# Reciprocal root on Pool: one power instruction and one Newton step in place of the bit trick and three steps

## The chip, the cores and the metric

The kernel runs on one core of a Trainium2 chip. The metric is the device time of one execution in microseconds (us). A trace covers a little less than that: the span of the profiled execution of the kernel before is 319.7 us, its time 321.52. A ratio is the mean time of one kernel's fast runs over that of the other's of the same rounds, so it is not quite the ratio of the medians that stand beside it.

## The reference

```python
x: [8, 1024, 2048] float32; gamma, beta: [2048]; eps = 1e-5
mean = np.mean(x, axis=-1, keepdims=True)
var = np.var(x, axis=-1, keepdims=True)
out = gamma * (x - mean) / np.sqrt(var + eps) + beta
return 0.5 * out * (1 + np.tanh(np.sqrt(2 / np.pi) * (out + 0.044715 * out ** 3)))
```

There are 8192 rows, so 64 tiles of 128 rows. x is 67.1 MB and the output is as large.

## The kernel before

The tiles go through in 22 groups, the first of one tile and the others of three. One load brings a group (3 MiB), one store takes it away. Seven group buffers are loaded ahead. A later load goes out on the SyncE queue right after a store, when the store before that one has landed in memory, because it reuses that buffer (in the trace of before SyncE waits for such a landing 14 times, 125.0 us in all).

```python
def scalar_var(i):                   # first tile of a group: statistics on ScalarE
    sq = gsmall.tile([P, 1], F32, name="sq")
    nc.scalar.activation(out=junk, in_=xts[i], func=ACTF.Square, bias=slot(i)[:, 0:1], accum_out=sq, ...)
    nc.gpsimd.tensor_scalar(out=slot(i)[:, 1:2], in0=sq, scalar1=1.0 / d, scalar2=None, op0=MUL)   # L136

def group_chain(g):                  # 1/sqrt(var + eps) and sqrt(var + eps) of three tiles, on Pool
    po = nc.gpsimd
    po.tensor_scalar(out=ve, in0=mvs[g][:, :, 1], scalar1=float(eps), scalar2=None, op0=ADD)
    po.tensor_scalar(out=y[:].bitcast(I32), in0=ve[:].bitcast(I32), scalar1=-0.5,
                     scalar2=float(0x5F3759DF), op0=MUL, op1=ADD)
    for _ in range(3):               # Newton: y = y * (1.5 - 0.5 * ve * y * y)
        po.tensor_tensor(out=t, in0=y, in1=y, op=MUL)
        po.tensor_tensor(out=t, in0=t, in1=ve, op=MUL)
        po.tensor_scalar(out=t, in0=t, scalar1=-0.5, scalar2=1.5, op0=MUL, op1=ADD)
        po.tensor_tensor(out=y, in0=y, in1=t, op=MUL)
    po.tensor_tensor(out=std, in0=ve, in1=y, op=MUL)

def diagonal(j): ...                 # ScalarE: w = identity * std, waits for the chain (L160)
def affine(j): ...                   # VectorE: ps = (x - mean) * gamma (L166); TensorE: ps += w @ beta (L169)
def gelu(j): ...                     # ScalarE: x = gelu(y * ps) (L178), then the store (L186; last group L184, L181)
```

The other two tiles of a group get their statistics on VectorE (`bn_stats`, L123). VectorE's statistics of later groups stand in program order between the affine instructions of earlier ones.

Of the kernel before, what the change touches and what calls it, by code (L numbers as in the profile page):

```python
# [7 lines left out]
F32 = mybir.dt.float32  # L8
BF16 = mybir.dt.bfloat16
I32 = mybir.dt.int32  # L10
ACTF = mybir.ActivationFunctionType
MUL = mybir.AluOpType.mult
ADD = mybir.AluOpType.add
SUB = mybir.AluOpType.subtract
P = 128
# [4 lines left out]
def kernel(  # L20
# [10 lines left out]
    nc = tc.nc  # L31
# [8 lines left out]
    singles = ctx.enter_context(tc.tile_pool(name="singles", bufs=1))  # L40
# [12 lines left out]
    for b, i in enumerate(starts):  # L53
        m = R if i else 1
# [25 lines left out]
    for b in range(NB):  # L80
# [6 lines left out]
    ident = singles.tile([P, P], F32)  # L87
    nc.gpsimd.affine_select(out=ident, in_=ones, pattern=[[-1, P]], base=0, channel_multiplier=1,
                            compare_op=mybir.AluOpType.is_equal, fill=0.0)
    H = d // 2  # L90
    halves = [slice(h * H, (h + 1) * H) for h in range(2)]
    ps = [[psum.tile([P, H], F32, name=f"ps{k}{h}") for h in range(2)] for k in range(2)]
    for pts, row in zip(ps, (g_t, b_t)):
        for pt, s in zip(pts, halves):
            for c in range(0, H, BANK):
                nc.tensor.matmul(pt[:, c:c + BANK], lhsT=ones[0:1, :],  # L96
# [41 lines left out]
    def group_chain(g):  # L138

        m = groups[g]  # L140
        ve = gsmall.tile([P, m], F32, name="ve")
        y = gsmall.tile([P, m], F32, name="y")
        t = gsmall.tile([P, m], F32, name="t")
        std = gsmall.tile([P, m], F32, name="std")
        po = nc.gpsimd
        po.tensor_scalar(out=ve, in0=mvs[g][:, :, 1], scalar1=float(eps), scalar2=None, op0=ADD)  # L146
        po.tensor_scalar(out=y[:].bitcast(I32), in0=ve[:].bitcast(I32), scalar1=-0.5,  # L147
                         scalar2=float(0x5F3759DF), op0=MUL, op1=ADD)
        for _ in range(3):
            po.tensor_tensor(out=t, in0=y, in1=y, op=MUL)  # L150
            po.tensor_tensor(out=t, in0=t, in1=ve, op=MUL)  # L151
            po.tensor_scalar(out=t, in0=t, scalar1=-0.5, scalar2=1.5, op0=MUL, op1=ADD)  # L152
            po.tensor_tensor(out=y, in0=y, in1=t, op=MUL)  # L153
        po.tensor_tensor(out=std, in0=ve, in1=y, op=MUL)  # L154
        rstds[g] = (y, std)

# [6 lines left out]
    def affine(j):  # L163
        g, k = of_tile[j]
        for pt, s in zip(ps[j % 2], halves):
            nc.vector.scalar_tensor_tensor(out=pt, in0=xts[j][:, s], scalar=mvs[g][:, k, 0:1],  # L166
                                           in1=g_t[:, s], op0=ADD if j in on_scalar else SUB, op1=MUL)
            for c in range(0, H, BANK):
                nc.tensor.matmul(pt[:, c:c + BANK], lhsT=wts[j], rhs=b_t[:, s.start + c:s.start + c + BANK],  # L169
# [28 lines left out]
    for j in range(ntiles):  # L198
        g, k = of_tile[j]
        target = min(len(chunks), max(pos, done_at[g] + AFTER[k]))  # L200
        while pos < target:
            i, c = chunks[pos]
            chunk(i, c)
            pos += 1
            h = of_tile[i][0]
            if done_at[h] == pos:
                while passes and of_tile[passes[0][1]][0] <= h:
                    f, q = passes.pop(0)
                    f(q)
                group_chain(h)  # L210
        if k == 0:
            for q in range(groups[g]):
                diagonal(j + q)
        affine(j)
        if j > 0:
            gelu(j - 1)
        now = of_tile[chunks[min(pos, len(chunks) - 1)][0]][0]
        if passes and of_tile[passes[0][1]][0] <= now and k != 1:
            f, q = passes.pop(0)
            f(q)  # L220
# [36 lines left out]
```

## Time and profile before

| | before |
|---|---|
| median of the first runs | 321.75 us (321.65 to 321.97, 4 runs) |
| bytes moved | 134.38 MB, 420 GB/s over the span |
| chain of fifteen Pool instructions | 7.95 us |
| pace of compute, one group of three tiles | 13.33 us |
| last load landed | 274.5 us |
| last gelu ends | 311.1 us |
| last store landed | 318.2 us |

One column of a view of windows needs care. The DMA share is a mean over the core's sixteen DMA engines, so a share below 1 doesn't say whether all of them had a pause or a few of them a long one.

### The profile page before, as it was taken

To read this page: it belongs to the slowest core of one execution; us is meant where nothing else is said; L and a number is where in the kernel's file an instruction comes from. 1 tells how busy PE (TensorE), PEld (TensorE's weight loads), DVE (VectorE), ACT (ScalarE), POOL (GpSimd) and SP (SyncE) were. 2 spreads that over 40 slices of the span, in tenths; PEclk is the share of its full clock that TensorE was granted. 3 is DMA by queue.
4 is the path that set the end of the run, shared out by engine and by line. 5 is a ranking of instruction groups with operands and counts; after the bars stand their busy time and mean duration, and the time that the engine had idled before them with its cause. 6 is when DMAs were issued, how large, how long until landed. Compare 5 with 4: busy or idle time off the path is not lost.

```text
span 319.7 us, 2374 instructions
## 1 busy us (share of the span) xinstructions
PE 253.1 (79%) x528; PEld 104.0 (33%) x528; DVE 269.1 (84%) x344; ACT 238.6 (75%) x282; POOL 149.6 (47%) x356
## 2 busy tenths in 40 slices
PE   5982979869896696968969869896696966869670
PEld 2421424324333242333424324333242322324230
DVE  2677799999999999999999999999999989798420
ACT  2363978869797696977968869797696976968560
POOL 0305346373463734637346383563835638365300
PEclk9998789997999999979989997999999999999995
DMA  7999999999999999999999999999999999999797
GB/s 297 442 427 440 440 406 397 430 439 424 440 421 431 431 437 437 418 434 423 437 434 424 434 434 427 433 427 437 422 443 421 428 441 427 439 418 431 308 424 315
DMA packets 7074, 134.38 MB, mean 420 GB/s; under 512 B 786, under 2 KB 786, under 8 KB 1042
## 3 DMA queue, kind: packets, MB, share of 16 engines
q1 hardware_dynamic: 7056, 134.22, 98.4%
q8 instruction: 4, 0.07, 0.1%
q14 instruction: 10, 0.08, 0.1%
q10 hardware_dynamic: 4, 0.02, 0.0%
HBM read 67.13 MB, written 67.11 MB: 420 GB/s over the span
## 4 chain that ended last, share of the span: by engine, by line
DMA 34%; POOL 30%; issue 26%; PE 3%; ACT 2%; DVE 1%; POOLq 0%; SPq 0%; ACTq 0%
DMA out_dram<-xt 26%; POOL t L152 10%; DMA xt<-in_x_dram 8%; POOL y L153 6%; POOL t L151 6%; PE ps L169 3%; POOL t L150 3%; ACT xt L178 2%; POOL mv L136 1%; POOL std L154 1%; POOL ve L146 1%; DVE st L123 1%; POOL y L147 1%; ACT w L160 1%; DVE ps L166 0%
## 5 line engine op out<-in xcount | busy, mean ns | idle before, releaser
L169 PE MATMUL ps<-b_t,w 128*128 128x512 f32 x512 | 239.1, 625 | 53.3 <-ACT w L160 52.4
L166 DVE SCALAR_TENSOR_TENSOR ps<-xt,mv,g_t 128x1024 f32<-128x1024 f32 x128 | 158.7, 1287 | 21.1 <-ACT xt L178 21.1
L169 PEld LDWEIGHTS ps<-b_t,w 128*128 128x128 f32 x512 | 98.8, 199 | 194.3 <-issue 101.2
L178 ACT ACTIVATE xt<-ps,y 128x1024 f32<-128x1024 f32 x128 | 134.4, 1107 | 9.6 <-PE ps L169 8.9
L123 DVE BATCH_NORM_STATS2 st<-xt 128x6 f32<-128x512 f32 x172 | 109.5, 670 | 12.1 <-DMA xt<-in_x_dram 12.1
L136 POOL TENSOR_SCALAR mv<-sq 128x1 f32<-128x1 f32 x21 | 5.5, 263 | 114.0 <-ACT junk L134 108.9
L160 ACT ACTIVATE w<-ident,std 128x128 f32<-128x128 f32 x64 | 21.1, 391 | 49.9 <-POOL std L154 49.9
L152 POOL TENSOR_SCALAR t<-t 128x3 f32<-128x3 f32 (+1 forms) x66 | 50.7, 767 | 5.8
L134 ACT ACTIVATE junk<-xt,mv 128x2048 fp8e5<-128x2048 f32 x21 | 41.9, 1993 | 0.1
L129 ACT ACTIVATE junk<-xt 128x2048 fp8e5<-128x2048 f32 x21 | 40.2, 1916 | 0.0
L153 POOL TENSOR_TENSOR y<-y,t 128x3 f32<-128x3 f32 (+1 forms) x66 | 32.2, 488 | 5.5
L151 POOL TENSOR_TENSOR t<-t,ve 128x3 f32<-128x3 f32 (+1 forms) x66 | 31.2, 473 | 5.2
L150 POOL TENSOR_TENSOR t<-y 128x3 f32<-128x3 f32 (+1 forms) x66 | 14.8, 224 | 5.3
L125 DVE BATCH_NORM_AGGREGATE mv<-st 128x2 f32<-128x24 f32 x43 | 11.3, 264 | 2.7
L96 PE MATMUL ps<-g_t,ones 1*128 1x512 f32 x8 | 7.2, 1072 | 3.5 <-DMA g_t<-in_gamma_dram 3.5
L146 POOL TENSOR_SCALAR ve<-mv 128x3 f32<-128x3 f32 (+1 forms) x22 | 5.2, 235 | 9.1 <-DVE mv L125 7.4
L96 PE MATMUL ps<-b_t,ones 1*128 1x512 f32 x8 | 7.0, 1056 | 0.0
L99 ACT ACTIVATE g_t<-ps 128x1024 f32<-128x1024 f32 x2 | 2.0, 1024 | 6.7 <-PE ps L96 6.7
L154 POOL TENSOR_TENSOR std<-ve,y 128x3 f32<-128x3 f32 (+1 forms) x22 | 5.2, 237 | 1.7
L99 ACT ACTIVATE b_t<-ps 128x1024 f32<-128x1024 f32 x2 | 2.0, 1024 | 4.8 <-PE ps L96 4.8
L147 POOL TENSOR_SCALAR y<-ve 128x3 int32<-128x3 int32 (+1 forms) x22 | 4.3, 197 | 1.8
L96 PEld LDWEIGHTS ps<-g_t,ones 1*128 1x128 f32 x8 | 2.5, 325 | 6.6 <-issue 6.6
(11 smaller groups left out, 13.4 us busy)
## 6 DMA issues: line engine op xcount, KB each, us to landing
xt<-in_x_dram SPq DMA_DIRECT2D x20, 3072.0 KB, 22.1
out_dram<-xt SPq DMA_DIRECT2D x20, 3072.0 KB, 21.3
xt<-in_x_dram SPq DMA_DIRECT2D x4, 1024.0 KB, 8.5
out_dram<-xt SPq DMA_DIRECT2D x3, 1024.0 KB, 15.3
out_dram<-xt SPq DMA_DIRECT2D x2, 512.0 KB, 7.6
g_t<-in_gamma_dram ACTq DMA_DIRECT2D x1, 8.0 KB
b_t<-in_beta_dram ACTq DMA_DIRECT2D x1, 8.0 KB
```

The lines of the kernel that those rows point to most:

```text
L96: nc.tensor.matmul(pt[:, c:c + BANK], lhsT=ones[0:1, :], rhs=row[0:1, s.start + c:s.start + c + BANK], start=True, stop=True)
L123: nc.vector.bn_stats(out=sts[i][:, c, :], in_=xts[i][:, c * BANK:(c + 1) * BANK])
L129: nc.scalar.activation(out=junk, in_=xts[i], func=ACTF.Identity, scale=-1.0 / d, accum_out=slot(i)[:, 0:1], saturate=False)
L134: nc.scalar.activation(out=junk, in_=xts[i], func=ACTF.Square, bias=slot(i)[:, 0:1], accum_out=sq, saturate=False)
L150: po.tensor_tensor(out=t, in0=y, in1=y, op=MUL)
L151: po.tensor_tensor(out=t, in0=t, in1=ve, op=MUL)
L152: po.tensor_scalar(out=t, in0=t, scalar1=-0.5, scalar2=1.5, op0=MUL, op1=ADD)
L153: po.tensor_tensor(out=y, in0=y, in1=t, op=MUL)
L160: nc.scalar.activation(out=w, in_=ident, func=ACTF.Identity, scale=rstds[g][1][:, k:k + 1])
L166: nc.vector.scalar_tensor_tensor(out=pt, in0=xts[j][:, s], scalar=mvs[g][:, k, 0:1], in1=g_t[:, s], op0=ADD if j in on_scalar else SUB, op ...
L169: nc.tensor.matmul(pt[:, c:c + BANK], lhsT=wts[j], rhs=b_t[:, s.start + c:s.start + c + BANK], start=False, stop=True, skip_group_check=True)
L178: nc.scalar.activation(out=xts[j][:, s], in_=pt, func=ACTF.Gelu_apprx_tanh, scale=rstds[g][0][:, k:k + 1])
```

## The change

Its intent: Pool is the pacemaker of compute, and fifteen dependent small instructions are long, so compute the root with seven.

```diff
+    power = singles.tile([P, 4], F32)
+    nc.gpsimd.memset(power, -0.5)
...
-        po.tensor_scalar(out=y[:].bitcast(I32), in0=ve[:].bitcast(I32), scalar1=-0.5,
-                         scalar2=float(0x5F3759DF), op0=MUL, op1=ADD)
-        for _ in range(3):
-            po.tensor_tensor(out=t, in0=y, in1=y, op=MUL)
-            po.tensor_tensor(out=t, in0=t, in1=ve, op=MUL)
-            po.tensor_scalar(out=t, in0=t, scalar1=-0.5, scalar2=1.5, op0=MUL, op1=ADD)
-            po.tensor_tensor(out=y, in0=y, in1=t, op=MUL)
+        po.tensor_tensor(out=y, in0=ve, in1=power[:, :m], op=mybir.AluOpType.pow)
+        po.tensor_tensor(out=t, in0=y, in1=y, op=MUL)
+        po.tensor_tensor(out=t, in0=t, in1=ve, op=MUL)
+        po.tensor_scalar(out=t, in0=t, scalar1=-0.5, scalar2=1.5, op0=MUL, op1=ADD)
+        po.tensor_tensor(out=y, in0=y, in1=t, op=MUL)
```

## The prediction

> **What bounds the kernel now.** I read the page first, then the windows, then the Pool and DVE timelines of one group in the middle, then the end. The page has no engine at its limit on average, but 420 GB/s over the whole span:
>
> ```profile
> PE 253.1 (79%) x528; PEld 104.0 (33%) x528; DVE 269.1 (84%) x344; ACT 238.6 (75%) x282; POOL 149.6 (47%) x356
> HBM read 67.13 MB, written 67.11 MB: 420 GB/s over the span
> ```
>
> An average hides stages, so next the windows (span, busy time and count of PE, PEld, DVE, ACT, POOL, then granted clock, DMA share, GB/s):
>
> ```profile
> 146.67:160.00 13.33, 12.02 (x28) 4.96 (x27) 12.55 (x17) 11.66 (x14) 7.01 (x17) 1.00 1.01 431
> 240.00:274.50 34.50, 26.29 (x60) 10.76 (x59) 30.76 (x41) 27.05 (x35) 18.03 (x42) 1.00 1.00 431
> 274.50:296.00 21.50, 18.18 (x42) 7.46 (x41) 19.24 (x22) 17.02 (x19) 12.61 (x24) 1.00 1.01 433
> 296.00:304.00 8.00, 5.42 (x13) 2.20 (x12) 3.69 (x4) 4.88 (x7) 2.23 (x9) 1.00 0.76 326
> 304.00:312.00 8.00, 5.94 (x14) 2.28 (x12) 1.82 (x2) 4.69 (x5) 0.00 (x0) 1.00 0.95 402
> 312.00:319.70 7.70, 0.00 (x0) 0.00 (x0) 0.00 (x0) 0.00 (x0) 0.00 (x0) 0.51 0.75 304
> ```
>
> The DMA engines are full until 296 us and move about 431 GB/s. After that they have holes. So the span is set by bytes, plus a start, plus holes near the end. The compute engines have their own pace underneath. The chain of waits shows it as one Pool instruction per group, always 13.33 us after the last one:
>
> ```profile
> 103.06 0.23 POOL mv L136
> 116.39 0.23 POOL mv L136
> 129.72 0.23 POOL mv L136
> 143.06 0.23 POOL mv L136
> ```
>
> This is a loop through the Pool: L136 needs ScalarE's variance pass, then come the fifteen instructions of the chain, then the three diagonals (0.98 us), two gelus (2.10) and the next variance pass (1.99) on ScalarE, in program order. From one group's last Pool instruction to the next L136 is 5.05 us in the chain of waits ("issue"), and the Pool part is the rest, about 8.3 us. Pool is thus the pacemaker of compute at 47% busy. But a group of three tiles moves 3 MiB in and 3 MiB out, 6.29 MB, and at 431 GB/s that takes 14.6 us. Compute at 13.33 us is faster than DMA. It lives on the seven blocks loaded ahead, and the whole-run list of waits has DVE waiting for loads only five times, 12.1 us in all, one of them of 1.94 us at 274.5 us, when the last load lands. After that only stores are left.
>
> The end is where compute shows. The DMA queue sees the last two full stores at
>
> ```profile
> 288.75 0.33 SPq L186 DMA_DIRECT2D out_dram<-xt  x1
> 301.94 0.33 SPq L186 DMA_DIRECT2D out_dram<-xt  x1
> ```
>
> 13.2 us apart, while a store of 3.15 MB drains in 7.3 us. About 8 MB of earlier stores is left at 274.5 us (17.5 MB moved after that, less 9.4 MB for the last three blocks), so the queue is dry near 274.5 + 18.6 + 7.3 = 300.4 us, before 301.94. That is the hole.
>
> [...]
>
> **The change, part by part.** One group of before on Pool, and the DVE instructions beside it:
>
> ```profile
> 117.01 0.20 POOL L147 TENSOR_SCALAR y<-ve 128x3 int32<-128x3 int32 x1
> 117.29 0.20 POOL L150 TENSOR_TENSOR t<-y 128x3 f32<-128x3 f32 x1
> 117.56 1.11 POOL L151 TENSOR_TENSOR t<-t,ve 128x3 f32<-128x3 f32 x1
> 118.76 1.11 POOL L152 TENSOR_SCALAR t<-t 128x3 f32<-128x3 f32 x1
> ...
> 121.90 1.27 POOL L152 TENSOR_SCALAR t<-t 128x3 f32<-128x3 f32 x1
> 123.25 1.11 POOL L153 TENSOR_TENSOR y<-y,t 128x3 f32<-128x3 f32 x1
> 124.44 0.20 POOL L154 TENSOR_TENSOR std<-ve,y 128x3 f32<-128x3 f32 x1
> ```
> ```profile
> 117.34 2.49 DVE L166 SCALAR_TENSOR_TENSOR ps<-xt,mv,g_t 128x1024 f32<-128x1024 f32 x2 [0.31 <-ACT xt L178]
> 121.84 2.47 DVE L166 SCALAR_TENSOR_TENSOR ps<-xt,mv,g_t 128x1024 f32<-128x1024 f32 x2
> ```
>
> An undisturbed instruction takes 0.20 us and starts 0.28 us after the one before. One that meets L166 takes 1.1 to 1.3 us. The chain starts at 116.69 us and ends at 124.64: 7.95 us = 15 x 0.28 (4.2) + four meetings at about 0.95 (3.8).
> - Removed: the bit trick and two Newton steps, nine instructions, of which two meet L166: 9 x 0.28 + 2 x 0.95 = 4.4 us. The later L166 pair is not met any more, because the chain is over by then.
> - Added: one power instruction of 128x3, taking P. [...] I take P = 1 us[...]. The memset of four columns runs once before the first data and costs nothing.
> - Sum: the chain is 7.95 - 4.4 + P = 4.5 us, about 3.4 us shorter. If P were about the 4.4 us removed, the change would be nil.
> - In the middle: the loop could now turn in about 9.9 us, but DVE has 12.55 us of work per group in the first window above (94%), so compute gains 0.5 us a group at most. Over 20 groups it catches up with the loads some groups earlier. It then waits for loads, because DMA needs 14.6 us. The 11 to 16 us that this seems to be worth do not reach the end: the last load still lands near 274.5 us.
> - At the end: two chains (those starting at 276.5 and 290.8 us) lie on the path from the last load to the last gelu (309.98 to 311.1). I take some 1.8 us out of the first, where DVE is next in line, and 3.4 less a little out of the second, so the last gelu moves about 4 us forward, to 307. The last full store moves from 301.94 to about 298, before the queue runs dry at 300.4. The holes then close: 8 x (1 - 0.76) = 1.9 us and 8 x (1 - 0.95) = 0.4 us, together 2.3 us. The drain after 312 us, with its share of 0.75, stays, as the last small stores must still land (7.6 us each on the page).
>
> So 321.66 - 2.3 is about **319.4 us**, 0.7% less.
>
> **Rivals.** First, the power instruction is slow. [...] While P stays under 4.4 us nothing is lost. Up to about 5.7 us the loop stays under DMA's 14.6 (13.33 + 1.3), and only the end suffers, perhaps 1 to 3 us, so 322 to 324. [...] Second, [...]L166 waits for Pool instead. DVE is 94% busy, so one more microsecond a group would put it at 13.6 us, still under 14.6; the middle hides it, and the end loses about 1 us of the gain: 320.5. Third, compute is the true bound and speeds up everywhere: 20 x 0.5 to 0.7 us would give about 308 to 312. The full DMA share up to 296 us speaks against it[...]. Fourth, the holes move instead of closing: with compute waiting for loads earlier, store order changes and the end is as empty as before: 321.5.
>
> **Range and chances.** The hole limits the gain to 2.3 us, with another 1 us if the drain shortens too; the second and fourth rivals cost the gain but little more. So 317.6 to 321.9 should hold it 8 times in 10. A gain of over 2% needs under 315.2, which only the third rival gives: 0.03. Over 2% slower needs P above some 6 us or a stalled DVE: 0.09. Within 2%: 0.88.
>
> **What would show it.** In the changed profile: seven Pool instructions a group, chain 4 to 5 us with the power at about 1 us; the 13.33 us spacing of L136 gone, shorter early and near 14.6 late; more DVE waiting on loads; the last load landing still within 1 us of 274.5; a DMA share over 0.9 from 296 to 304 us; the last gelu ending near 307. I am wrong if the power takes over 4.4 us, if the DVE affine instructions stretch, if a DMA hole appears before 290 us, or if the last load lands earlier than 272 us.

P = 1 us is a bare assumption. The forecast's sum keeps all its terms, 7.95 - 4.4 + 1 = 4.5 us for the chain and 321.66 - 2.3 = 319.4 us for the kernel, but the 1 us has no support, and part of the 0.09 for over 2% slower has none either.

## The result, and the profile after

The changed kernel took 322.69 us (median, 322.62 to 323.15, 4 runs) against 321.75 us before: ratio 1.0031, 95% interval 1.0014 to 1.0049. It counts as the same at the 2% line, as forecast at 0.88, but that class is wide enough to be met without the gain that I had argued for: the kernel is about 1 us slower where I had forecast 2.3 us faster. The result was correct.

The page of the changed kernel, the two lines that answer to the first ones of before:

```profile
PE 257.2 (80%) x528; PEld 101.8 (32%) x528; DVE 266.6 (83%) x344; ACT 238.8 (74%) x282; POOL 108.7 (34%) x181
HBM read 67.13 MB, written 67.11 MB: 418 GB/s over the span
```

Pool has 175 instructions and 41 us of busy time fewer, and the rate over the span has gone down. One group of the changed kernel on Pool, from the timeline (start, length, engine, line, operation, operands):

```profile
108.07 0.83 POOL L138 TENSOR_SCALAR mv<-sq 128x1 f32<-128x1 f32 x1 [6.09 <-ACT junk L136]
108.98 1.12 POOL L148 TENSOR_SCALAR ve<-mv 128x3 f32<-128x3 f32 x1
110.19 0.88 POOL L149 TENSOR_TENSOR y<-ve,power 128x3 f32<-128x3 f32 x1
111.14 1.30 POOL L150 TENSOR_TENSOR t<-y 128x3 f32<-128x3 f32 x1
112.52 1.12 POOL L151 TENSOR_TENSOR t<-t,ve 128x3 f32<-128x3 f32 x1
...
114.28 0.19 POOL L154 TENSOR_TENSOR std<-ve,y 128x3 f32<-128x3 f32 x1
120.56 0.82 POOL L138 TENSOR_SCALAR mv<-sq 128x1 f32<-128x1 f32 x1 [6.10 <-ACT junk L136]
```

L149 is the power: 0.88 us, beside 0.19 us for the multiply of L154, which has the same shape and meets nothing. The first group's power, of 128x1, took 0.58 us. The chain from L148 to the end of L154 is 114.47 - 108.98 = 5.5 us in place of 7.95. It is not the same everywhere: most chains up to 157 us take 5.5 us, those from 158 to 265 us mostly 3.9 to 4.6 us, and the last two 6.3 and 5.8 us. The next group's L138 comes 12.49 us later in place of 13.33: compute is faster. The windows of the changed kernel, columns as in the prediction:

```profile
146.67:160.00 13.33, 10.71 (x25) 4.12 (x23) 12.26 (x17) 11.76 (x14) 6.58 (x10) 1.00 1.01 433
240.00:274.50 34.50, 27.17 (x58) 10.72 (x56) 29.02 (x38) 25.53 (x34) 8.46 (x16) 0.95 1.01 432
274.50:296.00 21.50, 19.01 (x41) 7.91 (x40) 18.97 (x22) 16.39 (x19) 10.64 (x15) 0.92 1.01 432
296.00:304.00 8.00, 7.37 (x18) 3.04 (x17) 5.63 (x5) 6.10 (x8) 0.98 (x2) 1.00 0.91 390
304.00:312.00 8.00, 4.12 (x10) 1.52 (x8) 0.00 (x0) 3.46 (x4) 0.00 (x0) 0.98 0.95 403
312.00:321.00 9.00, 0.00 (x0) 0.00 (x0) 0.00 (x0) 0.00 (x0) 0.00 (x0) 0.50 0.51 208
```

The hole between 296 and 304 us has closed as forecast: 0.91 where it was 0.76. The last full store was issued earlier, as SyncE's timeline shows:

```profile
300.11 0.33 SPq L186 DMA_DIRECT2D out_dram<-xt  x1
```

That is 1.8 us before the 301.94 us of before, and the last gelu ends at 309.3 in place of 311.1 us, as its second half shows, first before, then in the changed kernel:

```profile
309.98 1.12 ACT L178 ACTIVATE xt<-ps,y 128x1024 f32<-128x1024 f32 x1 [0.60 <-PE ps L169]
```
```profile
308.16 1.11 ACT L178 ACTIVATE xt<-ps,y 128x1024 f32<-128x1024 f32 x1 [0.60 <-PE ps L169]
```

Nearly everything that I wanted to happen at the end did happen, and the span is 1.1 us longer. The lost time is in the last window, after 312 us, where only stores run. The DMA view of 310 to 321 us in 40 slices, first of before, then of the changed kernel (busy tenths, then GB/s):

```profile
DMA  9997999999989699996999999998000001000000
GB/s 387 447 387 298 417 387 477 477 477 417 417 357 447 268 477 477 477 447 268 372 447 372 432 402 372 462 387 358 30 0 0 0 0 30 0 0 0 0 0 0
```
```profile
DMA  9897999999889999999996333211110100000000
GB/s 417 357 447 298 387 477 447 447 447 417 357 357 462 402 372 417 432 372 387 447 402 253 149 134 134 104 74 75 60 60 30 45 15 0 0 0 0 0 30 0
```

Before, all sixteen engines work up to 317.7 us and stop together. In the changed kernel most stop at 315.8 us and a few go on alone for over 3 us: shares of 0.3, 0.2, 0.1. The mean was full, but the engines were not in step.

The trace also holds the times at which each transfer's sixteen parts reported (its semaphore records, read from the packed trace; no view of the profile shows them). In the traces a full transfer has sixteen such increments, and sixteen packets of 4 bytes beside its data (784 for the 49 transfers of more than one row in the kernel before). I read them as one from each of the sixteen engines, when its own share has landed. The lengths fit that: a full transfer has 128 packets of 24 KB, 0.91 us each, so a sixteenth of it is eight packets or 7.3 us, and its last report mostly comes 7.26 us after that of the transfer before. Sorted, for the stores of blocks 19 and 20 (in us; a block is the buffer of one group; 20 is the last that goes out in one store):

```
before, block 19: 299.4 299.7 299.8 299.9 300.0 300.0 300.0 300.8 301.0 301.3 302.2 302.2 302.7 302.8 303.6 303.6
before, block 20: 310.5 ...                                                                        310.8 310.9
after,  block 19: 299.6 299.8 299.9 299.9 299.9 300.0 300.0 300.4 301.0 301.1 302.3 302.6 303.0 303.4 304.4 304.7
after,  block 20: 308.7 (eight of them) ... 309.7 309.9 310.3 310.6 311.7 311.9
```

This is the explanation that the experiments then tested. Before, the block 20 store is issued at 301.94 us. The fast engines have been dry since about 300 us, and that is the hole in the mean. The slowest engine is busy with block 19 until 303.60 us and reports block 20 at 310.85: 7.25 us later, the ordinary time of one store. **It had no pause at all.** In the changed kernel the fast engines go on earlier, and the slowest goes from 304.67 to 311.94, 7.27 us. From its block 19 report to the very last report of the kernel is 14.64 us before and 14.67 us after. The records don't name the engines. That the same one comes last each time is inferred from its steps up to the end, which agree in both kernels within 0.02 us. So the hole's closing can't shorten the run; the end is where the slowest engine stands at block 19, plus 14.66 us.

### The profile page after: what moved, and what is told of

The parts are those of the page before. It is cut to its first block, busy times and chain, and to the rows that moved or that the text cites. A ratio compares the mean times of both kernels' runs of the same rounds, so it can differ in the third digit from the quotient of the medians.

```text
span 320.8 us, 2199 instructions
## 1 busy us (share of the span) xinstructions
PE 257.2 (80%) x528; PEld 101.8 (32%) x528; DVE 266.6 (83%) x344; ACT 238.8 (74%) x282; POOL 108.7 (34%) x181
## 4 chain that ended last, share of the span: by engine, by line
DVE 39%; DMA 25%; issue 17%; POOL 10%; PE 4%; ACT 2%; POOLq 0%; DVEq 0%; ACTq 0%; SPq 0%
DVE ps L166 22%; DMA xt<-in_x_dram 16%; DVE st L125 15%; DMA out_dram<-xt 9%; PE ps L169 4%; POOL y L149 2%; POOL t L151 2%; POOL t L152 2%; DVE mv L127 2%; ACT xt L178 1%; POOL t L150 1%; POOL ve L148 1%; POOL y L153 1%; POOL mv L138 1%; POOL std L154 0%
## 5 line engine op out<-in xcount | busy, mean ns | idle before, releaser
L169 PE MATMUL ps<-b_t,w 128*128 128x512 f32 x512 | 243.2, 626 | 47.1 <-DVE ps L166 41.3
L178 ACT ACTIVATE xt<-ps,y 128x1024 f32<-128x1024 f32 x128 | 136.9, 1108 | 49.8 <-PE ps L169 49.8
L166 DVE SCALAR_TENSOR_TENSOR ps<-xt,mv,g_t 128x1024 f32<-128x1024 f32 x128 | 158.0, 1281 | 6.6 <-ACT xt L178 6.6
L169 PEld LDWEIGHTS ps<-b_t,w 128*128 128x128 f32 x512 | 96.8, 198 | 194.3 <-issue 92.7
L125 DVE BATCH_NORM_STATS2 st<-xt 128x6 f32<-128x512 f32 x172 | 109.9, 673 | 27.2 <-DMA xt<-in_x_dram 27.2
L138 POOL TENSOR_SCALAR mv<-sq 128x1 f32<-128x1 f32 x21 | 10.7, 508 | 167.0 <-ACT junk L136 167.0
L149 POOL TENSOR_TENSOR y<-ve,power 128x3 f32<-128x3 f32 (+1 forms) x22 | 21.9, 995 | 1.8
L150 POOL TENSOR_TENSOR t<-y 128x3 f32<-128x3 f32 (+1 forms) x22 | 21.2, 962 | 1.7
L151 POOL TENSOR_TENSOR t<-t,ve 128x3 f32<-128x3 f32 (+1 forms) x22 | 21.1, 958 | 1.7
L148 POOL TENSOR_SCALAR ve<-mv 128x3 f32<-128x3 f32 (+1 forms) x22 | 15.1, 687 | 9.7 <-DVE mv L127 7.9
L152 POOL TENSOR_SCALAR t<-t 128x3 f32<-128x3 f32 (+1 forms) x22 | 8.0, 361 | 1.9
L153 POOL TENSOR_TENSOR y<-y,t 128x3 f32<-128x3 f32 (+1 forms) x22 | 6.1, 277 | 1.8
L154 POOL TENSOR_TENSOR std<-ve,y 128x3 f32<-128x3 f32 (+1 forms) x22 | 4.3, 193 | 1.7
```

The costliest lines, as they stand in the source:

```text
L125: nc.vector.bn_stats(out=sts[i][:, c, :], in_=xts[i][:, c * BANK:(c + 1) * BANK])
L149: po.tensor_tensor(out=y, in0=ve, in1=power[:, :m], op=mybir.AluOpType.pow)
L166: nc.vector.scalar_tensor_tensor(out=pt, in0=xts[j][:, s], scalar=mvs[g][:, k, 0:1], in1=g_t[:, s], op0=ADD if j in on_scalar else SUB, op ...
L169: nc.tensor.matmul(pt[:, c:c + BANK], lhsT=wts[j], rhs=b_t[:, s.start + c:s.start + c + BANK], start=False, stop=True, skip_group_check=True)
L178: nc.scalar.activation(out=xts[j][:, s], in_=pt, func=ACTF.Gelu_apprx_tanh, scale=rstds[g][0][:, k:k + 1])
```

## The experiments

**Where the tiles lie.** The kernel before with only the new tile and its memset.

```diff
+    power = singles.tile([P, 4], F32)
+    nc.gpsimd.memset(power, -0.5)
```

> The kernel before, fifteen-instruction chain and all, with only the tile of powers and its memset added[...]. If the 1 us that the change lost comes from where the tiles lie, or from the start, this kernel shows it: about 322.7 us, first load landing near 6.5 us. If it comes from the new chain or its timing: 321.7 us, first load near 5.9 us.

Measured: 322.23 us against 322.18 us before in the same job, ratio 0.9998 (0.9980 to 1.0016). The small loss does not come with the tile alone, and the first load landed at 5.7 us, not near 6.5. The kernel before itself ranged from 321.51 to 323.19 us over 11 runs, so part of the first 1 us is scatter.

**A still shorter chain.** The changed kernel without its Newton step.

```diff
-        po.tensor_tensor(out=t, in0=y, in1=y, op=MUL)
-        po.tensor_tensor(out=t, in0=t, in1=ve, op=MUL)
-        po.tensor_scalar(out=t, in0=t, scalar1=-0.5, scalar2=1.5, op0=MUL, op1=ADD)
-        po.tensor_tensor(out=y, in0=y, in1=t, op=MUL)
```

> The changed kernel without its Newton step: three Pool instructions a group, and the accuracy of the power alone. My theory: the end is set by the slowest of the sixteen DMA engines, which never idles in either kernel; the hole that I saw was the other engines waiting for it. Then a still shorter chain moves the last gelu forward by some 1 to 3 us and the time by nothing: 322.7 us, within 0.5. Rival, the hole in the mean share is what compute costs: each microsecond of an earlier last gelu is seen, 320 to 321.5 us.

Measured: 323.32 us, ratio 1.0032 (1.0014 to 1.0051). The outputs are right. The window of its end:

```profile
296.00:304.00 8.00, 8.00 (x20) 3.60 (x19) 5.76 (x5) 5.58 (x6) 0.00 (x0) 1.00 1.00 430
```

The DMA share is 1.00 and the last full store went out at 298.72 us, 3.2 us before that of the kernel before. No time came of it; the time is even a little above the 322.2 to 323.2 us that I had expected. The rival (a microsecond of earlier compute is a microsecond) is refuted. The slowest engine stood at 305.64 us after block 19, 2.04 us later than before, and the profiled time was 2.05 us longer (323.57 against 321.52).

**A longer chain.** The kernel before with four Newton steps.

```diff
-        for _ in range(3):
+        for _ in range(4):
```

> The kernel before with a fourth Newton step: nineteen instructions, a chain 1.1 to 2.1 us longer, a loop of 14.4 to 15.4 us. My theory: in the kernel before, the last full store is issued at 301.94 us, when the slowest engine is about to run dry (303.60), so there is no room in this direction, and the time rises by 2 to 6 us. Rival, compute is hidden anyway with room to spare: 321.7 us, within 0.5.

Measured: 343.13 us, ratio 1.0653 (1.0626 to 1.0681), 21 us slower. The direction was right and the size far off. The pace, from the timeline, and two windows:

```profile
108.41 0.22 POOL L136 TENSOR_SCALAR mv<-sq 128x1 f32<-128x1 f32 x1 [5.09 <-ACT junk L134]
122.84 0.22 POOL L136 TENSOR_SCALAR mv<-sq 128x1 f32<-128x1 f32 x1 [5.09 <-ACT junk L134]
```
```profile
240.00:274.50 34.50, 29.75 (x66) 12.38 (x64) 30.81 (x40) 27.17 (x31) 20.38 (x51) 0.95 1.00 431
274.50:296.00 21.50, 17.16 (x37) 7.13 (x36) 18.16 (x24) 16.08 (x22) 9.52 (x26) 0.92 0.62 265
```

The loop is 14.43 us, 1.10 us longer, and about 19 turns of it are the 21 us. I had held that a loop under DMA's 14.6 us a group is hidden. It isn't: DMA moves seven groups of input ahead of compute, so its loads are done at about 275 us whatever compute does, and then it waits for stores (share 0.62). The compute line adds up from the first group to the last on its own. In the kernel before that line ends where DMA's does: the sixteen reports of its last store lie between 318.00 and 318.24 us, no wider apart than in this kernel, where every engine waited for compute (338.82 to 339.04 us). The slowest engine sets the 318.24 us and had no pause, so **a faster chain could win nothing there**, and a slower one pays nearly in full.

**One engine made late.** The kernel before, plus one load of 23 rows that nobody reads.

```diff
     for b in range(NB):
         load(b)
+    extra = singles.tile([P, d], F32)
+    nc.sync.dma_start(out=extra[0:23, :], in_=xf[0:23, :])
```

> The kernel before with one more load after the first seven blocks: 23 rows of x into a tile that nobody reads. [...]all 23 packets of 8 KB should go to one engine, 23 x 0.309 = 7.1 us of its time, though it is 0.14% of the bytes. If the end follows the mean of the sixteen engines: 0.44 us more, 322.1 us. If it follows the slowest one: the time rises by 7.1 us less the lead of that engine over the slowest, so by 3 to 7 us, 324.6 to 328.8 us; and the last landings of the late engine are alone at the end.

Measured: 327.90 us, ratio 1.0173 (1.0153 to 1.0194), 5.7 us slower for 0.14% more bytes. The mean of the engines would have given 0.44 us. By this run's profile page the extra load brings 24 packets (7098 in place of 7074), one of them under 512 B (787 in place of 786), where a full transfer has sixteen of those: its 23 rows went to one engine, as I read it. In the trace one report alone is late, 8.8 us behind the first right after the extra load, 5.6 us behind through the rest (block 19: 309.7 us, the next slowest at 307.3).

The same 23 rows in the changed kernel:

> The changed kernel with the same 23 rows on one engine. In the kernel before they cost 5.6 us. If the end is the slowest engine's in the changed kernel too, they cost 7.1 us less that engine's lead over the slowest, so 3 to 7 us over the changed kernel: ratio to before 1.012 to 1.024. If compute in the changed kernel ran far enough ahead to hide a late engine: ratio 1.003.

Measured: 327.95 us, ratio 1.0182 (1.0164 to 1.0200), about 5 us more than the changed kernel's repeat below. Compute, though further ahead, doesn't hide a late engine.

**The power twice.** The changed kernel with the power instruction issued a second time.

```diff
         po.tensor_tensor(out=y, in0=ve, in1=power[:, :m], op=mybir.AluOpType.pow)
+        po.tensor_tensor(out=y, in0=ve, in1=power[:, :m], op=mybir.AluOpType.pow)
```

> The changed kernel with its power instruction issued twice: the chain is longer by 0.9 to 1.3 us in every group. My theory: the changed kernel's compute is ahead of the slowest DMA engine (last full store issued at 300.1 us, that engine free at 304.7), so the time does not move: ratio to before 1.003, within 0.002. Rival, the power costs the microsecond that was lost: 324 us or more, ratio 1.006 or more.

Measured: 322.86 us against 322.22, ratio 1.0016 (0.9995 to 1.0037). A power more in every group costs nothing that can be seen, so the power's length is not what was lost.

**Which part of the run.** The new chain in the last two groups only, then in all but the last two (the edit is shortened here).

```diff
+        if g >= len(groups) - 2:     # the other kernel: g < len(groups) - 2
             (power and one Newton step)
+        else:
+            (bit trick and three Newton steps)
```

> The fifteen-instruction chain in the first twenty groups and the new chain in the last two only: the middle keeps the pace of 13.33 us, the end has the shorter chain. By the step of my prediction, closing the hole after 296 us is worth 2 us: ratio 0.993. By the slowest-engine theory it is worth nothing: ratio 1.000, within 0.002. If the early pace of the middle is what makes the changed kernel slower, this kernel also shows it by not being slower than before.

> The reverse: the new chain in the first twenty groups, the old one in the last two. If the small loss comes from the middle, where compute now runs ahead of the loads: ratio 1.003, as for the whole change. If the loss comes from the end: ratio 1.000.

Measured: the end alone 322.44 us, ratio 1.0010 (0.9992 to 1.0028); the middle alone 322.99 us, ratio 1.0025 (1.0005 to 1.0044). The first is the clean test of my step about the hole. Its window at the end:

```profile
296.00:304.00 8.00, 7.37 (x18) 3.12 (x17) 5.64 (x5) 6.03 (x8) 1.05 (x2) 1.00 0.95 406
```

The hole is closed (0.95), the middle is the old one, and the 2 us do not come. The two ratios lie on the sides expected if the middle makes the small loss, but their intervals overlap, so this is a hint and no more.

**Instruction fetches.** The profile pages list two DMA queues of the kind "instruction", q8 and q14 (4 and 10 packets in the kernel before). I take their packets for fetches of the engines' programs. Each of these traces has 11 to 17 of them between 27 and 302 us: four of 16 KB, 0.9 to 1.1 us long, and seven to thirteen of 8 KB, mostly 0.31 us long. If a fetch holds up the data on the DMA engine that it runs on, fetches could be what makes the late engine late. Two kernels tested that.

```diff
             nc.sync.dma_start(out=dst, in_=blocks[b][:, :dst.shape[1], :])
+            for _ in range(64):
+                nc.sync.nop(nofuse=True)
```

> The changed kernel with 64 empty instructions on SyncE after each of 21 stores[...], put where SyncE waits for the landing of a store anyway. If the lag of the slowest DMA engine comes from instruction fetches that share it, there are some ten more fetches in the trace, one engine falls 3 us or more further behind at those times, and the time rises by 0 to 4 us (0 if that engine was not among the late ones). If fetches have no part in it: lag and time as in the changed kernel, ratio 1.003.

This one failed as an experiment: its trace has the same instructions on SyncE and the same 12 fetches as the changed kernel, so the empty instructions never reached the chip. (Five more fetches for the 704 instructions of the next kernel would make about ten for 1344.) It serves as a repeat of the changed kernel: 322.70 us, ratio 1.0019 (1.0001 to 1.0038). The second has instructions that stay:

```diff
         po.tensor_tensor(out=std, in0=ve, in1=y, op=MUL)
+        for _ in range(32):
+            po.memset(idle, 0.0)
```

> The run with empty instructions turned out to hold none (they were dropped before the chip: same instruction counts and same fetches as the changed kernel), so it was a second timing of the changed kernel. Here the padding is real: 32 memsets of one column on Pool after each group's chain, 704 instructions[...], some five more fetches of 8 KB. If fetches make the late engines late, five more delays of 0.3 to 0.7 us fall on one engine and the time rises by 0 to 3 us, ratio 1.003 to 1.010. If they don't matter: ratio 1.002, as the changed kernel. Either way the last store's end should be 14.66 us after the slowest landing of the store of block 19.

Measured: 323.61 us, ratio 1.0050 (1.0033 to 1.0068). The queue lines of the pages, the changed kernel and the padded one (packets, MB, share):

```profile
q14 instruction: 9, 0.07, 0.1%
```
```profile
q14 instruction: 14, 0.11, 0.1%
```

Five fetches more, and 0.6 to 1.0 us over the two timings of the changed kernel (the ratios differ by 0.0019 and 0.0031, of 322 us). The last store of the padded kernel was again bound by the late engine. That fits fetches as one source of the lag. It doesn't prove it, because the 704 memsets are also work on Pool's side (69.7 us busy). The reports of nine traces (the first nine rows of the table below) say a little more. Between 60 and 305 us the last report of a full transfer mostly comes 7.26 us after that of the transfer before; 22 of 304 such steps were over 0.5 us longer. A fetch ran during 14 of these 22, and during 84 of all 304. So late steps go with fetches more often than by chance, but eight had none: in the changed kernel the slowest engine lost 0.70 us before 187.8 us, with no fetch between 143.4 and 201.8 us. Fetches are at most a part of the lag.

**All traces together.** First and slowest report of block 19's store, the kernel's last report, its distance from the slowest, and the time of that same execution (us):

```
                     first   slowest   last     distance  time
before               299.43  303.60    318.24   14.64     321.52
changed              299.58  304.67    319.34   14.67     322.62
tile only            299.50  304.86    319.52   14.66     322.81
no Newton            299.49  305.64    320.30   14.65     323.57
power twice          299.70  304.85    319.50   14.65     322.78
changed, repeat      299.64  304.72    319.38   14.67     322.68
new chain at end     299.74  304.75    319.41   14.66     322.68
new chain in middle  299.78  304.34    319.00   14.66     322.28
padding              299.79  305.77    320.36   14.59     323.66
four Newton steps    317.05  317.21    339.04   21.83     342.31
```

In nine traces the distance is the same within 0.1 us, and the time follows the slowest engine, whatever the chain was. (The two kernels with the extra load are left out, because their late engine is the one that was made late; their distances are 14.66 us too.) Only the kernel whose compute was too slow (last row) leaves the rule; there the engines are in step, because all of them waited.

## Why the prediction was wrong

By its own steps:

- **The power's cost.** Taken as 1 us, measured 0.88 us in 18 of the 21 groups of three and 1.7 to 1.9 us in the other three. Right, with luck: the working behind it held a guess.
- **The chain.** Taken as 4.5 us, measured 5.5 us in most groups up to 157 us, about 4.5 us in many later ones, and 6.3 and 5.8 us in the two at the end, on which the forecast rested. The term mis-sized is the meetings with L166: I kept two. In the group shown above L148, L150 and L151 took 1.12 to 1.30 us each, and in the last group L151, L152 and L153 took about 1.1 us each: a third meeting, at my own 0.95 us, is the missing microsecond. A shorter chain starts at another moment of VectorE's program and need not meet less of it.
- **The middle.** That VectorE would hold the pace was right: the turn is 12.49 us from 58 to 158 us, with VectorE busy for 12.35 us of it, and longer after that, when it waits for loads. The gain of "0.5 us a group at most" was too small by my own figures, 13.33 - 12.55 = 0.78 us; measured 0.84 us. More waiting for loads came true as well: 27.2 us in 12 waits in place of 12.1 us in 5. The last load landed at 275.6 us, just outside my 274.5 within 1 us.
- **The end.** The two chains there became 1.6 and 2.0 us shorter and not 1.8 and 3.4, so the last gelu moved 1.8 us and not 4, the last full store to 300.1 and not 298 us. Still enough: the hole closed.
- **The step that failed** is "The holes then close: 8 x (1 - 0.76) = 1.9 us and 8 x (1 - 0.95) = 0.4 us, together 2.3 us". I took the missing share as time of the whole kernel. It was idle time of the fast engines, which were waiting for a store while the slowest was still at work. That engine had no pause (7.25 us from block 19 to block 20, as in the changed kernel), so closing the hole could win nothing. The kernel with the new chain at the end alone showed the closed hole without the gain. The same step's "The drain after 312 us ... stays" failed with it: the idle time of the fast engines moved there, much as my fourth rival had it (at 321.5), though not by a changed order of stores. And 0.75 was no hole of before: the share is 0.95 from 312 to 318 us and 0.02 in the 1.7 us after that, when the last store had landed.
- **A rival's size.** I wrote that a chain longer by up to 1.3 us is hidden in the middle and costs 1 to 3 us. A loop longer by 1.10 us cost 21 us. Comparing 13.33 with 14.6 us a group was wrong, because DMA's loads run ahead and the two lines meet only at the end.
- **The small loss.** The two timings give ratios of 1.0031 and 1.0019. Shown is that the time follows the slowest engine's lag, 4.2 us in the trace before and 4.6 to 6.2 us in the traces with the new chain in the middle. But two kernels with the old middle also had 5.4 and 5.0 us (the extra tile alone, and the new chain at the end), so one trace a kernel doesn't settle it. Neither the added tile nor the power's length showed an effect. Fetches may be a part of the lag, but the changed kernel has one fetch fewer than before, so their number doesn't explain the difference between the two. Whether its lag is larger on average, and why, stays open.

No version here beats the kernel before. The arithmetic doesn't touch what the late engine has to carry, and no run here tried to give it less.

## What to carry to other kernels

Where DMA is full, ask of a hole in its mean share which engines were idle in it: here only a pause of the slowest one would have been time to be won, and the spread of a transfer's partial completions told that it had none. Before shortening one of two lines that run side by side (compute that depends on itself from group to group, and transfers), find where each ends alone; if they end together, one direction costs everything and the other gives nothing. A share of busy time of 47% said nothing about Pool: it paced compute, and making it faster was still worth nothing, while making its turn 1.10 us slower cost 21 us.
